# A diffusion trunk's layer on one core: the queries made beside the q/kv projection, in areas shared with its input

## The chip, the cores and the metric

One core of a Trainium2 chip runs the whole program. The time is device microseconds from start to end of one execution; the median of several runs is what is compared. The profile is one more execution, recorded by the hardware profiler. Engines: TensorE (PE, matmuls; its weight loads are listed as PEld), VectorE (DVE), ScalarE (ACT), GpSimd (POOL) and SyncE (SP, which issues nearly all DMAs). Each engine runs its own list of instructions in order and waits for others at semaphores.

## The reference

One layer for 1024 latent tokens and 128 context tokens (9 tiles of 128 tokens, 8 of them latent), width 1024. The tokens are normalised and modulated to `h`, one input projection feeds two groups of heads, and the part that matters here is the second, a latent attention with 4 heads:

```python
h = _rmsnorm(x, norm_g) * (1 + scale) + shift
u, v, g_a, c_q, c_kv, k_rope, g_b = _split_in(h @ w_in)
...
q = (_rmsnorm(c_q, q_norm_g) @ w_uq).reshape(B, L, MLA_HEADS, QK_NOPE + QK_ROPE)
ckv = _rmsnorm(c_kv, kv_norm_g)
...
logits.append(jnp.einsum('bqhn,bkhn->bhqk', qn, kn) + jnp.einsum('bqhr,bkr->bhqk', qrb, kr))
```

`c_q` has 256 columns, `c_kv` 128 and `k_rope` 64: together the 448 columns of the q/kv projection. Everything is computed in float32.

## The kernel before

The work runs in stages. **Front:** `x` is transposed and modulated; `hh` and `hl` hold the result, tokens in columns, by block `k` of 128 channels (8) and group `g` of three token tiles (384 columns). Each float32 matmul is done in three passes, for which a matrix is split into a part rounded for the fast format (`..h`, by ACT or POOL) and the rest (`..l`, by DVE, `lo_of`, L105). **Channel stage:** twelve blocks of the input projection for the gates and the first group of heads. **q/kv projection** (from L804 on): for each token tile `t` the 24 matmuls of L812 to L814 make `zacc` in one PSUM bank. `z_stats` (L767) then has ACT square (L772, L773) and copy it (L774), DVE work out the reciprocal root in some fifteen operations on two columns (L776, L777, then `rsqrt`, L115 to L125) and POOL rotate the key part. `cq_transpose` (L797) brings the previous tile's `c_q` to columns and `fold` (L746, tiles 2 to 5) multiplies two query weights of a head into one. **Query stage** (from L829 on): `q_nope(g, h)` (6 matmuls of 384 columns), `q_rope(t)` (6 of 256), `q_rope_T(t)` (4 transposes) and `keys` (transposes of key tiles) write the query areas `q` and the key tiles. **Attention** (from L953 on) and the **output projection** follow.

From the query stage on, the order on each engine is the program's own: a block under `tc.manual_schedule` keeps the order in which the instructions are written. `run` executes a step's matmuls at once and moves a counted clock on by the step's cost; `later(dt, fn)` sets an eviction aside until that clock has passed `dt`, and `need` brings it forward when a step depends on it. So the costs in the code only set the order. The q/kv loop before is not under such a block.

PSUM has 8 banks: `psa` hands out six in turn (tag "acc": `zacc`, `qn`, `qr`, some `qrT`), `pst` two (tag "t": `cqT`, `fold`, `kT`, other `qrT`). A step that takes a bank waits until the bank's last user has been read out.

In SBUF `hh` and `hl` are 48 tiles of 384 columns in the pool `ht`. When the q/kv projection is done the pool is closed, and three query pools of the same size in sum (`qp0` to `qp2`) and the key pool `kv` are opened in its place and in that of `w1`. Late in the attention, `qp0` makes room for a pool `wo` with the first pieces of the output weights and the tiles `mh`, `ml` of the output stage; the other pieces lie in `qp1` and `qp2`.

```python
for t in range(NT):
    ...
    z_stats(t, ps)
    if FT <= t < FT + 4:
        fold(t - FT)
    if t > 0:
        cq_transpose(t - 1)
```

Of the kernel before, what the change touches and what calls it, by code (L numbers as in the profile page):

```python
# [9 lines left out]
F32 = mybir.dt.float32  # L10
# [77 lines left out]
def tile_hymba_step(ctx: ExitStack, tc: tile.TileContext, I, O):  # L88
# [115 lines left out]


# [540 lines left out]
    def fold(h):  # L746
# [20 lines left out]
    def z_stats(t, ps):  # L767
# [3 lines left out]
        j1 = sm.tile([P, 256], BF16, tag="j1", name=f"j1{t}", bufs=1)  # L771
        S.activation(j1, ps[:, 0:256], AF.Square, accum_out=ssz[:, 0:1])  # L772
        S.activation(j1[:, :128], ps[:, 256:384], AF.Square, accum_out=ssz[:, 1:2])  # L773
        S.copy(zs, ps[:, :448])  # L774
        v = sm.tile([P, 2], F32, tag="zv", name=f"zv{t}")
        V.tensor_scalar(v[:, 0:1], ssz[:, 0:1], 1.0 / 256.0, EPS, op0=ALU.mult, op1=ALU.add)  # L776
        V.tensor_scalar(v[:, 1:2], ssz[:, 1:2], 1.0 / 128.0, EPS, op0=ALU.mult, op1=ALU.add)  # L777
        r = rsqrt(sm, v, 2, "z")
        V.tensor_scalar(scl[:, t : t + 1], r[:, 0:1], ATTN_SCALE, None, op0=ALU.mult)
        V.tensor_scalar(nscl[:, t : t + 1], r[:, 0:1], -ATTN_SCALE, None, op0=ALU.mult)  # L780
        V.scalar_tensor_tensor(kvn[:, t, :], zs[:, 256:384], r[:, 1:2], kvg, op0=ALU.mult, op1=ALU.mult)
        kr = zs[:, 384:448]
        if t < NS:
# [22 lines left out]
    for t in range(NT):  # L806
# [9 lines left out]
        if FT <= t < FT + 4:  # L816
            fold(t - FT)
# [716 lines left out]
```

## Time and profile before

| | us |
|---|---|
| Median of 3 runs (lowest, highest) | 637.11 (632.85, 637.33) |
| Profiled execution, its own time | 638.64 |
| Span of the profile | 636.9 |
| Busy: PE, DVE, ACT, POOL | 616.1, 361.3, 256.0, 186.3 |

The profiled execution's own time is 1.7 us longer than its span: what lies before the first and after the last instruction. Matmuls are pipelined and their ends are modelled, so two of them overlap in the list, and the start of one to the start of the next is its pitch. The q/kv projection starts at 253.4 us, the query stage at 300.5 and the scores at 330.7. An `idle before` names what released the engine. [...]

### The profile page before, as it was taken

What the parts mean: (1) busy time and instruction counts of PE and PEld (TensorE: products, weight loads), DVE (VectorE), ACT (ScalarE), POOL (GpSimd) and SP (SyncE); (2) the same over time, 40 slices, a digit from 0 to 9 for tenths busy, and PEclk for the clock granted to TensorE, in tenths of its full rate; (3) what the DMA queues carried; (4) which work ended last, traced back from release to release, by engine and by line L of the source; (5) the groups of instructions that cost most, each with busy time, mean ns of one, the idle gap of its engine ahead of it and who ended that gap; (6) DMA issues with size and microseconds to landing.
All of it is one profiled execution on the core that took longest, in us unless ns stands there. A gap on an engine that the chain in (4) does not pass through costs nothing.

```text
span 636.9 us, 9914 instructions
## 1 busy us (share of the span) xinstructions
PE 616.1 (97%) x3715; PEld 557.1 (87%) x3715; DVE 361.3 (57%) x922; ACT 256.0 (40%) x613; POOL 186.3 (29%) x219
## 2 busy tenths in 40 slices
PE   7799999999999999999979999999999999999995
PEld 6577889999999999999968899999999988888884
DVE  4427446236866200566876666777667765387655
ACT  4355784012111111333765655555655542232222
POOL 3534202355436510222753222332222341000001
PEclk9799999999999999999989999999999999999998
DMA  8866200015023430000000000001101112523311
GB/s 321 331 229 217 66 1 2 1 42 205 20 97 113 127 116 0 25 15 1 7 2 1 1 1 9 26 1 35 34 1 34 33 67 69 198 99 133 105 61 66
DMA packets 17119, 46.32 MB, mean 73 GB/s; under 512 B 1952, under 2 KB 6448, under 8 KB 17072
## 3 DMA queue, kind: packets, MB, share of 16 engines
q1 hardware_dynamic: 16928, 45.51, 20.6%
q8 instruction: 29, 0.48, 0.3%
q10 hardware_dynamic: 144, 0.20, 0.1%
q14 instruction: 18, 0.15, 0.1%
HBM read 40.87 MB, written 4.83 MB: 72 GB/s over the span
## 4 chain that ended last, share of the span: by engine, by line
PE 89%; DVE 3%; DMA 2%; issue 2%; ACT 2%; SPq 1%; POOL 0%; ACTq 0%; DVEq 0%
PE tp L618 6%; PE tp L151 6%; PE tp L152 6%; PE tp L153 6%; PE pT L1046 5%; PE w L1303 5%; PE w L1304 5%; PE w L1305 5%; PE s L999 3%; PE s L1000 3%; PE s L1002 3%; PE o L1072 3%; PE s L1001 3%; PE o L1070 3%; PE s L1003 3%; PE o L1071 3%
## 5 line engine op out<-in xcount | busy, mean ns | idle before, releaser
L990 POOL TENSOR_SCALAR e<-e,rs 128x1280 f32<-128x1280 f32 x32 | 42.8, 1339 | 139.4 <-DVE rs L989 123.7
L105 DVE TENSOR_TENSOR pl<-pT,ph 128x512 fp32r<-128x512 f32 x81 | 55.5, 687 | 47.6 <-ACT ph L1050 47.4
L153 PE MATMUL tp<-hh,w2l 128*128 128x384 f32 x216 | 72.6, 336 | 0.0
L152 PE MATMUL tp<-hl,w2h 128*128 128x384 f32 x216 | 72.6, 336 | 0.0
L151 PE MATMUL tp<-hh,w2h 128*128 128x384 f32 x216 | 72.6, 336 | 0.0
L984 ACT ACTIVATE e<-s,nb,scl 128x256 f32<-128x256 f32 x64 | 56.1, 881 | 39.2 <-DVE nb L978 39.1
L1050 ACT CAST ph<-pT 128x512 fp32r<-128x512 f32 x80 | 45.4, 589 | 44.0 <-PE pT L1046 39.0
L1046 PE MATMUL pT<-ident,e 128*128 128x128 f32 x320 | 47.9, 273 | 0.7 <-DVE pl L105 0.7
L1070 PE MATMUL o<-ph,vh 128*128 128x256 f32 x160 | 47.3, 296 | 0.0
L105 DVE TENSOR_TENSOR w2l<-w2r,w2h 128x1024 fp32r<-128x1024 f32 x12 | 20.2, 1687 | 43.8 <-POOL w2h L108 43.8
L1072 PE MATMUL o<-ph,vl 128*128 128x256 f32 x160 | 44.7, 279 | 0.0
L1071 PE MATMUL o<-pl,vh 128*128 128x256 f32 x160 | 44.6, 278 | 0.0
L999 PE MATMUL s<-kch,q 128*128 128x512 f32 (+2 forms) x100 | 39.5, 395 | 2.1 <-DVE q L105 2.1
L974 DVE TENSOR_REDUCE m<-s 128x1 f32<-128x1024 f32 x32 | 38.9, 1216 | 4.4 <-PE s L1003 4.4
L1046 PEld LDWEIGHTS pT<-ident,e 128*128 128x128 f32 x320 | 37.5, 140 | 4.4 <-DVE pl L105 1.5
L151 PEld LDWEIGHTS tp<-hh,w2h 128*128 128x128 f32 x216 | 40.6, 188 | 0.6
L152 PEld LDWEIGHTS tp<-hl,w2h 128*128 128x128 f32 x216 | 40.6, 188 | 0.2
L153 PEld LDWEIGHTS tp<-hh,w2l 128*128 128x128 f32 x216 | 40.6, 188 | 0.0
L1000 PE MATMUL s<-kcl,q 128*128 128x512 f32 (+2 forms) x100 | 35.9, 359 | 0.0
L1002 PE MATMUL s<-krh,q 128*128 128x512 f32 (+2 forms) x100 | 35.7, 357 | 0.0
L1001 PE MATMUL s<-kch,q 128*128 128x512 f32 (+2 forms) x100 | 35.7, 357 | 0.0
L1003 PE MATMUL s<-krl,q 128*128 128x512 f32 (+2 forms) x100 | 35.5, 355 | 0.0
(301 smaller groups left out, 1620.0 us busy)
## 6 DMA issues: line engine op xcount, KB each, us to landing
ada<-in_ada_ss SPq DMA_DIRECT2D x16, 512.0 KB, 11.1
w2r<-in_w_t SPq DMA_DIRECT2D x12, 512.0 KB, 3.8
xr<-in_x SPq DMA_DIRECT2D x9, 512.0 KB, 4.9
adag<-in_ada_g SPq DMA_DIRECT2D x8, 512.0 KB
wor<-in_w_o SPq DMA_DIRECT2D x8, 512.0 KB, 3.2
out_y<-y SPq DMA_DIRECT2D x8, 512.0 KB, 3.1
x<-in_x SPq DMA_DIRECT2D x6, 512.0 KB, 8.7
wvr<-in_w_v SPq DMA_DIRECT2D x8, 256.0 KB, 7.4
```

The costliest lines, as they stand in the source:

```text
L105: V.tensor_tensor(lo, src, f32(hi), op=ALU.subtract)
L151: T.matmul(ps, wh, xh, start=j == 0, stop=False)
L152: T.matmul(ps, wh, xl, start=False, stop=False)
L153: T.matmul(ps, wl, xh, start=False, stop=j == n - 1)
L984: S.activation(e[:, sl], src, AF.Exp, bias=nb, scale=scl[:, t : t + 1], accum_out=su[:, i : i + 1])
L999: T.matmul(ps, qh_, kch[:, sl], start=True, stop=False)
L1000: T.matmul(ps, qh_, kcl[:, sl], start=False, stop=False)
L1001: T.matmul(ps, ql_, kch[:, sl], start=False, stop=False)
L1046: T.transpose(ps[:, w : w + P], es[t, h][:, c * P : (c + 1) * P], ident)
L1070: T.matmul(o, vh[:, kt, :], ph[:, sl], start=c == 0, stop=False)
L1071: T.matmul(o, vh[:, kt, :], pl[:, sl], start=False, stop=False)
L1072: T.matmul(o, vl[:, kt, :], ph[:, sl], start=False, stop=c == n - 1)
```

## The change

Three tiles `area0` to `area2` replace the 48 tiles: `hh[k, g]` and `hl[k, g]` are columns of `area[g]`, and the queries of group `g` are written over them, once the q/kv projection has read the three tiles of the group. The query pools are gone, and the output weights and `mh` later lie in the same areas. The q/kv loop is put under `manual_schedule` and cut into eight steps of three matmuls (`z_chunk`); `merged` deals a second list in between by cost: `q_rope(t - 2)`, one or two `q_nope`, `cq_transpose(t - 1)`, `fold(t - 1)` (tiles 1 to 4), `q_rope_T(t - 3)`. What is left runs after the loop in a written order. In `z_stats` the copy comes ahead of the squares, and all of it is set aside by `later`. The warm-up of Exp's table (`warm_e`) is no longer tied to its place behind the query stage.

```diff
-    hh, hl = {}, {}
-    for k in range(NK):
-        for g in range(3):
-            hh[k, g] = ht.tile([P, GW], F32R, tag=f"hh{k}{g}", name=f"hh{k}{g}")
-            hl[k, g] = ht.tile([P, GW], F32R, tag=f"hl{k}{g}", name=f"hl{k}{g}")
+    area = [ht.tile([P, 16, GW], F32R, tag=f"area{g}", name=f"area{g}") for g in range(3)]
+    hh = {(k, g): area[g][:, 2 * k, :] for k in range(NK) for g in range(3)}
+    hl = {(k, g): area[g][:, 2 * k + 1, :] for k in range(NK) for g in range(3)}
...
+        def copies():
+            j1 = sm.tile([P, 256], BF16, tag="j1", name=f"j1{t}", bufs=1)
+            S.copy(zs, ps[:, :448])
+            S.activation(j1, ps[:, 0:256], AF.Square, accum_out=ssz[:, 0:1])
+            S.activation(j1[:, :128], ps[:, 256:384], AF.Square, accum_out=ssz[:, 1:2])
...
+        later(0.3, copies)
+        later(0.9, rope_key)
+        later(1.6, scales)
...
-        q = qpool[g].tile([P, 4, 4, GW], F32R, tag="q", name=f"q{g}")
+    for g in range(3):
+        q = area[g].rearrange("p (s h) c -> p s h c", s=4)
         qnh[g], qnl[g], qr[g] = q[:, 0], q[:, 1], q[:, 2:4]
...
+    NOPES = {4: [(0, 0)], 5: [(0, 1), (0, 2)], 6: [(0, 3)], 7: [(1, 0), (1, 1)], 8: [(1, 2), (1, 3)]}
     with tc.manual_schedule(engines=engines):
...
+        warm_e = sm.tile([P, 1], F32, tag="warm", name="warm_e", bufs=1)
+        S.activation(warm_e, ones[:, 0:1], AF.Exp)
+        rope_weights()
+        for t in range(NT):
+            beside = []
             if t >= 2:
-                run((0.43, lambda: q_rope_T(t - 2)))
...
+                beside.append((0.75, lambda t=t: q_rope(t - 2)))
+            beside += [(1.05, lambda n=n: q_nope(*n)) for n in NOPES.get(t, [])[:1]]
+            if t >= 1:
+                beside.append((0.25, lambda t=t: cq_transpose(t - 1)))
+            if 1 <= t < 5:
+                beside.append((0.45, lambda t=t: fold(t - 1)))
+            if t >= 3:
+                beside.append((0.45, lambda t=t: q_rope_T(t - 3)))
+            beside += [(1.05, lambda n=n: q_nope(*n)) for n in NOPES.get(t, [])[1:]]
+            merged([(0.62, lambda t=t, k=k: z_chunk(t, k)) for k in range(NK)], beside)
+        closed(c_w1)
+        c_kv, kv = opened("kv", side="left")
...
+        for cost, fn in (
+            (0.45, lambda: keys(0, 4, 0)),
+            (0.75, lambda: q_rope(7)),
+            (0.45, lambda: keys(0, 4, 1)),
+            (0.45, lambda: q_rope_T(6)),
+            (0.25, lambda: cq_transpose(8)),
+            (0.45, lambda: keys(4, 4, 0)),
+            (0.45, lambda: keys(4, 4, 1)),
+            (0.75, lambda: q_rope(8)),
+            (1.05, lambda: q_nope(2, 0)),
+            (0.45, lambda: q_rope_T(7)),
+            (1.05, lambda: q_nope(2, 1)),
+            (0.15, lambda: keys(8, 1, 1)),
+            (1.05, lambda: q_nope(2, 2)),
+            (0.15, lambda: keys(8, 1, 0)),
+            (1.05, lambda: q_nope(2, 3)),
+            (0.25, lambda: q_rope_T(8)),
+        ):
+            run((cost, fn))
         catch_up(1e9)
-    warm_e = sm.tile([P, 1], F32, tag="warm", name="warm_e", bufs=1)
-    tc.keep_in_program_order(S.activation(warm_e, ones[:, 0:1], AF.Exp))
...
-            mh[t] = wo.tile([P, 8, P], F32R, tag="mh", name=f"mh{t}", bufs=2)
+            mh[t] = flat[0][4 + len(mh) % 2].rearrange("p (c q) -> p c q", c=8)
```

Here is PE's list at the head of token tile 3 before the change (a name's first number is its tile; `hh01` is block 0 of group 1):

```order
L812 MATMUL zacc3_2634<-qh0_1654,hh01_114 128x448
L813 MATMUL zacc3_2634<-ql0_1655,hh01_114 128x448
L814 MATMUL zacc3_2634<-qh0_1654,hl01_115 128x448
L812 MATMUL zacc3_2634<-qh1_1786,hh11_120 128x448
L813 MATMUL zacc3_2634<-ql1_1787,hh11_120 128x448
L814 MATMUL zacc3_2634<-qh1_1786,hl11_121 128x448
```

And the same place after it:

```order
L937 MATMUL zacc3_2589<-qh0_1609,area1_113 128x448
L938 MATMUL zacc3_2589<-ql0_1610,area1_113 128x448
L939 MATMUL zacc3_2589<-qh0_1609,area1_113 128x448
L151 MATMUL qr1_2600<-wrh_2377,cqh_2373 128x256 [waits Activation_49]
L152 MATMUL qr1_2600<-wrl_2378,cqh_2373 128x256
L153 MATMUL qr1_2600<-wrh_2377,cql_2374 128x256 [waits DVE_49]
```

`q_rope(1)` (`qr1`, six matmuls, three shown) has moved from the query stage to behind the first three matmuls of tile 3, and with it a wait for DVE's `cql`.

PE's list at the end of the query stage, before (`qn23` is `q_nope` of group 2, head 3; `s100` the first scores):

```order
L151 MATMUL qn23_3413<-cqh_2418,wfh_2420 128x384
L152 MATMUL qn23_3413<-cql_2419,wfh_2420 128x384
L153 MATMUL qn23_3413<-cqh_2418,wfl_2421 128x384
L888 MATMUL qrT8_3424<-ident_75,qun8_3371 128x128 [waits DVE_49,PE_49,Activation_49]
L888 MATMUL qrT8_3424<-ident_75,qun8_3371 128x128
L999 MATMUL s100_3453<-kch_3061,q0_3067 128x512 [waits DVE_49]
L1000 MATMUL s100_3453<-kcl_3062,q0_3067 128x512
```

PE's list behind the first keys and `q_rope(7)` of the new tail (`kT00`, `kT01` are the two kinds of key tiles 0 to 3, `kT40`, `kT41` of 4 to 7):

```order
L917 MATMUL kT01_3243<-ident_75,krd_2386 128x128 [waits PE_49]
L917 MATMUL kT01_3243<-ident_75,krd_2386 128x128 x3
L897 MATMUL qrT6_3260<-ident_75,qr16_3133 128x128 [waits Pool_49]
L897 MATMUL qrT6_3260<-ident_75,qr16_3133 128x128
L897 MATMUL qrT6_3260<-ident_75,qun6_3119 128x128 x2
L836 MATMUL cqT8_3268<-ident_75,z8_3200 128x128 [waits DVE_49]
L836 MATMUL cqT8_3268<-ident_75,z8_3200 128x128
L917 MATMUL kT40_3273<-ident_75,kvn_2385 128x128 [waits DVE_49]
L917 MATMUL kT40_3273<-ident_75,kvn_2385 128x128 x3
L917 MATMUL kT41_3285<-ident_75,krd_2386 128x128 [waits DVE_49]
L917 MATMUL kT41_3285<-ident_75,krd_2386 128x128 x3
```

The keys, which stood among `q_nope` and `q_rope` before, now follow each other and `cqT8`; `kT01`, `cqT8`, `kT40` and `kT41` take the two banks of `pst` in turn, the last three with a wait for DVE.

DVE's list where the second keys are read out, before (`zr`, `scl`, `kvn` belong to the statistics of tile 8):

```order
L105 TENSOR_TENSOR kcl_3062<-kT00_3103,kch_3061 128x512 [waits Activation_49]
L125 SCALAR_TENSOR_TENSOR zr_3015<-zt_3016,zr_3015 128x2 [waits DVE_49]
L872 TENSOR_TENSOR qr11_3130<-qr1_3109,rope_2424 128x256 [waits Activation_49]
L779 TENSOR_SCALAR scl_92<-zr_3015 128x1 [waits DVE_49]
L780 TENSOR_SCALAR nscl_93<-zr_3015 128x1
L781 SCALAR_TENSOR_TENSOR kvn_2436<-z8_3006,zr_3015,kvg_162 128x128
L105 TENSOR_TENSOR q0_3067<-qn02_3121,q0_3067 128x384 [waits Activation_49]
L105 TENSOR_TENSOR krl_3064<-kT01_3136,krh_3063 128x512 [waits Activation_49]
```

And after:

```order
L124 TENSOR_TENSOR zt_3237<-zt_3237,zw_3238 128x2 [waits DVE_49]
L105 TENSOR_TENSOR krl_3209<-kT01_3243,krh_3208 128x512 [waits Activation_49]
L125 SCALAR_TENSOR_TENSOR zr_3236<-zt_3237,zr_3236 128x2 [waits DVE_49]
L123 TENSOR_TENSOR zt_3237<-zr_3236 128x2 [waits DVE_49]
L907 TENSOR_TENSOR area2_114<-qrT6_3260,area2_114 64x4x128 [waits PE_49,Activation_49]
L105 TENSOR_TENSOR cql_2374<-cqT8_3268,cqh_2373 128x2x128 [waits PE_49]
```

Before, the statistics of tile 8 end ahead of `krl`; now six of their operations stand between `kcl` and `krl` and two more behind `krl`, ahead of a half of `q_rope_T(6)`'s read-out and of `cql`.

## Rows read from the trace of the kernel before

**Rows 1.** Page, part 1: busy time, share of the span, instructions of each engine

```profile
PE 616.1 (97%) x3715; PEld 557.1 (87%) x3715; DVE 361.3 (57%) x922; ACT 256.0 (40%) x613; POOL 186.3 (29%) x219
```

**Rows 2.** Windows: length, busy us (instructions) of each engine, PE clock, DMA share, GB/s

```profile
260.00:300.00 40.00, 40.00 (x213) 37.22 (x212) 26.09 (x148) 12.79 (x52) 10.90 (x40) 1.00 0.06 16
300.00:320.00 20.00, 19.94 (x143) 19.06 (x142) 16.83 (x45) 15.85 (x38) 13.88 (x28) 1.00 0.02 6
320.00:340.00 20.00, 16.10 (x91) 13.95 (x91) 14.01 (x26) 10.38 (x22) 7.02 (x11) 0.91 0.00 1
```

**Rows 3.** Timeline of PE, 324 to 335: start, us, engine, line, operation [idle before <-releaser]

```profile
324.41 0.34 PE L153 MATMUL qn<-cqh,wfl 128*128 128x384 f32 x1
326.25 0.41 PE L888 MATMUL qrT<-ident,qr 128*128 128x128 f32 x2 [1.50 <-DVE q L898]
...
327.60 0.34 PE L153 MATMUL qn<-cqh,wfl 128*128 128x384 f32 x1
328.25 0.41 PE L888 MATMUL qrT<-ident,qun 128*128 128x128 f32 x2 [0.31 <-DVE q L898]
330.74 0.57 PE L999 MATMUL s<-kch,q 128*128 128x512 f32 x1 [2.08 <-DVE q L105]
...
334.48 0.39 PE L1003 MATMUL s<-krl,q 128*128 128x512 f32 x1
334.71 0.28 PE L999 MATMUL s<-kch,q 128*128 128x256 f32 x1
```

**Rows 4.** Windows, PE alone, 331 to 332: length, busy, granted clock, DMA

```profile
331.00:332.00 1.00, 1.00 (x4) 0.51 0.00 0
```

**Rows 5.** Timeline of PE, end of token tile 0 and the query stage

```profile
258.10 0.37 PE L814 MATMUL zacc<-qh,hl 128*128 128x448 f32 x1
258.31 0.36 PE L812 MATMUL zacc<-qh,hh 128*128 128x448 f32 x1
...
311.88 0.36 PE L151 MATMUL qr<-wrh,cqh 128*128 128x256 f32 x1
...
312.68 0.34 PE L151 MATMUL qn<-cqh,wfh 128*128 128x384 f32 x1
...
313.73 0.27 PE L907 MATMUL kT<-ident,kvn 128*128 128x128 f32 x1
...
314.19 0.36 PE L151 MATMUL qr<-wrh,cqh 128*128 128x256 f32 x1
```

**Rows 6.** Timeline of ACT, first token tile's statistics

```profile
258.51 0.38 ACT L772 ACTIVATE j<-zacc 128x256 bf16<-128x256 f32 x1 [4.39 <-PE zacc L814]
...
259.28 0.53 ACT L774 COPY z<-zacc 128x448 f32<-128x448 f32 x1
259.69 0.52 ACT L761 ACTIVATE wrh<-rraw,cst 128x256 fp32r<-128x256 f32 x1
```

**Rows 7.** Groups by line, DVE, 253.4 to 331: count, busy us, mean ns, idle before

```profile
L898 DVE TENSOR_TENSOR q<-qrT,q 64x512 fp32r<-64x512 f32 x16 | 11.0, 689 | 0.4
...
L123 DVE TENSOR_TENSOR zt<-zr 128x2 f32<-128x2 f32 x27 | 5.7, 212 | 0.9
...
L105 DVE TENSOR_TENSOR cql<-cqT,cqh 128x256 fp32r<-128x256 f32 x9 | 3.8, 418 | 0.4
...
L105 DVE TENSOR_TENSOR kcl<-kT,kch 128x512 fp32r<-128x512 f32 x2 | 1.4, 681 | 0.0
```

**Rows 8.** Groups by line, ACT, the same stretch

```profile
L910 ACT CAST kch<-kT 128x512 fp32r<-128x512 f32 x2 | 1.2, 587 | 0.0
```

**Rows 9.** Timeline, table load, end of the first exponential, third head's scores

```profile
329.45 1.28 ACT L952 ACT_TABLE_LOAD   x1
...
330.75 0.20 ACT L952 ACTIVATE warm_e<-ones 128x1 f32<-128x1 f32 x1
...
338.40 0.20 ACT L984 ACTIVATION_READ_ACCUMULATOR e<-s,nb,scl 128x1 f32 x1
...
340.46 0.40 PE L999 MATMUL s<-kch,q 128*128 128x512 f32 x1
```

More of the change, by code (lines that the diff above doesn't have):

```diff
@@ L203, in run, with merged @@
         now[0] += step[0]
+    def merged(a, b):
+        ta, tb = sum(x for x, _ in a) or 1.0, sum(x for x, _ in b) or 1.0
+        ia = ib = 0
+        da = db = 0.0
+        while ia < len(a) or ib < len(b):
+            if ib >= len(b) or (ia < len(a) and da / ta <= db / tb):
+                da += a[ia][0]
+                run(a[ia])
+                ia += 1
+            else:
+                db += b[ib][0]
+                run(b[ib])
+                ib += 1
     c_pc, pc = opened("pc", side="right")
@@ L876, in raw @@
             made.add(("r", t))
-        later(0.75, raw)
+        later(0.85, raw)
     def q_rope_T(t):
@@ L883, in q_rope_T @@
         srcs = rot[t]
-        tp = (pst if t >= TP else psa).tile([P, 512], F32, tag="t" if t >= TP else "acc", name=f"qrT{t}")
+        late = t == NS
+        tp = (pst if late else psa).tile([P, 512], F32, tag="t" if late else "acc", name=f"qrT{t}")
         for s_, src in enumerate(srcs):
@@ L931, in tile_hymba_step @@
[L931 to L949 removed]
+        pool_copy(vh[:, vs_, :], kvn[:, vs_, :])
@@ new lines, in values, with z_chunk @@
+        G.tensor_tensor(vl[:, vs_, :], kvn[:, vs_, :], f32(vh[:, vs_, :]), op=ALU.subtract)
+    zps = {}
+    def z_chunk(t, k):
+        g, j = t // 3, t % 3
+        sl = slice(j * P, (j + 1) * P)
+        if k == 0:
+            zps[t] = psa.tile([P, 512], F32, tag="acc", name=f"zacc{t}")
+        ps = zps[t]
+        a, b = hh[k, g][:, sl], hl[k, g][:, sl]
+        T.matmul(ps[:, :448], a, wqh[k], start=k == 0, stop=False)
+        T.matmul(ps[:, :448], a, wql[k], start=False, stop=False)
+        T.matmul(ps[:, :448], b, wqh[k], start=False, stop=k == NK - 1)
+        if k == NK - 1:
+            z_stats(t, ps)
@@ L1093, in value_steps @@
         return ns, tr, av, fin1, fin2
-    def merged(a, b):
-        ta, tb = sum(x for x, _ in a) or 1.0, sum(x for x, _ in b) or 1.0
-        ia = ib = 0
-        da = db = 0.0
-        while ia < len(a) or ib < len(b):
-            if ib >= len(b) or (ia < len(a) and da / ta <= db / tb):
-                da += a[ia][0]
-                run(a[ia])
-                ia += 1
-            else:
-                db += b[ib][0]
-                run(b[ib])
-                ib += 1
     woh, wol = {}, {}
+    flat = []
+    for g in range(3):
+        cols = area[g].rearrange("p a c -> p (a c)")
+        flat.append([cols[:, n * 1024 : (n + 1) * 1024] for n in range(6)])
     his, los = [], []
@@ L1317, in tile_hymba_step @@
             if 2 * c + LEAD + 1 == 11:
[L1318 removed]
                 c_wo, wo = opened("wo", side="left")
                 for k in range(2):
[L1321 removed]
+                    wo_piece(k, *flat[0][2 * k : 2 * k + 2])
                 mix_jobs(8)
```

183 lines of the change are left out of this document (72 added, 111 removed).

## The prediction, as written before the changed kernel was run

> **What bounds the kernel now.** Read the page first: TensorE (PE) is busy 97% of the span, the vector engine (DVE) 57% [rows 1]. So a change that keeps PE's work can give back only time in which PE waits or runs slowly. The windows say where that is in the stages the change touches: in 260 to 300 us PE is never idle and DVE is busy 26.1 of 40 us; in 300 to 320 DVE rises to 16.8 of 20; in 320 to 340 PE is idle 3.9 us and its granted clock falls to a mean of 0.91 [rows 2]. The timeline of PE, last, gives the places and, in brackets, what ended each wait: DVE's subtractions (L898, L105) all three times. I count from start to start, since ends are modelled. A query matmul has a pitch of 1.05/6 = 0.175 (six from 312.68 to 313.73 [rows 5]), a transpose 0.46/5 = 0.092 (five from 313.73 to 314.19). The gaps [rows 3]:
> 324.41 to 326.25 is 1.84, less 0.175: 1.66 waited.
> 327.60 to 328.25 is 0.65, less 0.175: 0.48.
> 328.25 to 330.74 is 2.49, less two transposes: 2.31.
> Sum 4.45 us. Then the first ten score matmuls, 330.74 to 334.71, take 3.97 us, though the tenth takes 0.23 (334.48 to 334.71), so ten should take 2.3: 1.67 us lost. [...] Everything that this change can win is thus 4.45 + 1.67 = 6.1 us, 1.0% of the span. [...]
>
> **What the change removes.** Eight of the twelve q_nope, seven of the nine q_rope and six of the nine q_rope_T go in front, between the q/kv matmuls. PE's instructions are the same ones, so PE's own work is unchanged. DVE's work is spread: a tile of the new loop holds on PE 24 q/kv matmuls at 0.21 (258.10 to 258.31 [rows 5]), one q_rope (0.80, 311.88 to 312.68), two q_nope (2.1) and six transposes (0.55), 8.5 us; on DVE some 15 small operations at 0.2, a rotation of 256 columns (taken as the 256-column row, 0.42), two q_nope subtractions (bounded by 0.42 and 0.68 of the 256- and 512-column rows), cql 0.42 and two rotation subtractions at 0.69 [rows 7]: about 6.3 us. DVE keeps up there. The three waits above therefore go, 4.45 us.
>
> **What it adds: waits in the new tail.** After the last q/kv matmul PE still has six key transposes, q_rope 7 and 8, the q_nope of group 2 and three q_rope_T. The order shows three of these waiting for DVE through the two transposing banks (pst). Let T be the start of keys(0,4,0).
> ScalarE (ACT): the last q/kv matmul starts at T - 0.21, its copy 0.41 later (258.10 to 258.51 [rows 5, 6]), at T + 0.20. The copy now stands first (259.28 to 259.69, 0.41) and the two squares behind it (258.51 to 259.28, 0.77), so the cast of the first keys starts at T + 1.38 and ends at 1.97 (0.587 [rows 8]). DVE's kcl takes 0.681 [rows 7]: T + 2.65. PE got there at 0.37 + 0.80 + 0.37 + 0.37 = 1.91, so cq_transpose(8), which needs that bank, waits 0.74.
> DVE goes on in its order: rotation of q_rope(7) 0.42 (3.07), six small operations of tile 8's statistics at 0.2 (4.27), krl 0.68 (4.95). keys(4,4,0) needs that bank; PE was ready at 2.65 + 0.18 = 2.83 and waits 2.12.
> Then two small operations (5.35), half a rotation subtraction 0.69 (6.04), cql 0.42 (6.46). keys(4,4,1) waits for it; PE was ready at 4.95 + 0.37 = 5.32 and waits 1.14.
> Sum 4.0 us. Behind the waiting PE stand q_rope(8) and four q_nope, then the scores; by then (some 6 us of PE work later) DVE has the bank of the first scores free, so nothing is added there. I bound this sum from below at 0.7 (only the first wait, if the small operations slip in while DVE waits for ACT) and from above at 5.5 (ACT another 1.5 us late) and take 4.0, since every term is a row.
>
> **Other edits.** cq_transpose(0) comes after 3 matmuls of tile 1: PE is there 0.84 after the last matmul of tile 0 starts, the copy ends 0.41 + 0.53 = 0.94 after it [rows 5, 6], a wait of 0.1. The folds move one tile ahead; their loads stand on SP in the same order and behind the same buffers, freed by the q/kv weight splits of the stage before, so they cost nothing unless such a load is late; then the first fold would wait for it. The shared areas are followed by region: the writes of the input wait for the same instructions as before, and the queries of a group are written after its three tiles. Context and values on POOL go behind the tail, and are wanted only by the scores' third part and the value product: hidden. The Exp warm-up is hoisted to ACT's first instruction, where Silu's load then evicts it, so the 1.28 us load at 329.45 goes to the first exponential of the softmax [rows 9]. There the end of that exponential (338.40 + 0.20 = 338.60) had 1.86 us before the third head's scores at 340.46 that reuse its bank. The load fits: 0.
> [...]
>
> **The sum.** Waits 4.45 fall to 4.1: 0.35 us. And the clock? The new tail waits 4.0 of the 4.55 us from T + 1.91 to T + 6.46, at least as long and as dense as the stretch that ended in the window at 0.51 [rows 3, 4]. I take it that the clock falls again, only over q_rope(8) and q_nope instead of over the scores: 1.67 lost there as here.
> [...]
> So the profiled execution would go from 638.64 (636.9 of span and 1.7 around it) to 638.3. That execution lies 1.5 above the median; on the median the forecast is 637.11 - 0.35, about 636.8.
>
> **Rivals.**
> No dip: same waits, but the clock stays at full, because two groups of transposes break them. For it: the wait of 1.66 at 324 was not followed by slow work (326.25 to 327.60 holds four transposes and five query pitches, 0.37 + 0.88, at about full pace [rows 3]). Against it: the density above. 636.8 - 1.7 = 635.1.
> No late tail: ACT and DVE, freed of the backlog, have their casts ready, and only the 0.1 and the 0.7 stay. For it: DVE is busy only 26 of 40 us before [rows 2]. Against it: the chain cast, subtraction, bank is a latency, and an idle DVE does not shorten it. 637.11 - 6.1 + 0.8 = 631.8.
> Late third head: the Exp load in the softmax takes more than its 1.28 us, so that the 1.86 us in hand are overdrawn. At twice the row that is 2.56 - 1.86 = 0.7 us, 637.5. For it: nothing in the trace. Against it: an operation follows its load at once (329.45 + 1.28 to 330.75 [rows 9]). [...]
> Slower: DVE's subtraction of the transposed cq stands behind tile statistics (15 small operations and one longer, 3.0 us), and q_rope at the head of the tile after next waits for it. Place: tile 7, where 9 matmuls and 4 transposes lie between, 2.2 us, for 0.41 + 0.41 + 0.42 of eviction, a margin of 1.0; elsewhere (12 matmuls, a q_nope, 4 transposes: 3.9) 2.6. It decides from where DVE is over 1.0 us behind. Price if it is behind by one whole chain: 2.0 there and 0.4 in four other tiles, 3.6. For it: the engines keep their program order. Against it: 6.3 us of DVE work in 8.5. 636.8 + 3.6 = 640.4.
> That nothing is interleaved is excluded by the order.
>
> **Chances.** Forecast 0.42, no dip 0.25, no late tail 0.15, late third head 0.03, slower 0.15. The three runs before lie from 632.85 to 637.33, 0.7% apart, so 1% (6.4 us) is about what a measurement can tell from no change. For the range: the low end takes in the rival at 631.8 with 0.8 us for such scatter, 631.0; the high end stops at 639.6, which leaves most of the slower rival, some 0.1, outside. Faster by over 1% needs under 630.7: only a part of the no-late-tail case, 0.06. Slower by over 1% needs over 643.5: more than one chain late, 0.04. Between: 0.90.
>
> **What would show it.** Right: PE waits at cq_transpose(8), keys(4,4,0) and keys(4,4,1) of about 0.7, 2.1 and 1.1 us, released by DVE; no wait at the first score; the window behind them at the 0.5 level and the first scores at a pitch of 0.23; the Exp load ahead of the first exponential, with no wait of the third head. Wrong: waits of q_rope in the loop, released by DVE's cql; tail waits under 1 us; or an attention stage that has grown.

## The result, and the profile after

The changed kernel is slower: 640.11 us median of 20 runs (636.51 to 641.19) beside 637.46 of the kernel before (20 runs). The ratio is 1.0043 (95% interval 1.0027 to 1.0059), +2.7 us (1.7 to 3.8). It was forecast at 636.8, range 631.0 to 639.6: the time lies above that range, and the sign is the other one. The profiled execution took 639.19 us, with a span of 637.4.

Page, part 1, of the changed kernel (answers to [rows 1]):

```profile
PE 616.1 (97%) x3715; PEld 557.5 (87%) x3715; DVE 367.3 (58%) x922; ACT 259.3 (41%) x614; POOL 186.3 (29%) x219
```

PE's busy time is the same to the tenth of a microsecond (it counts matmuls at half clock at their longer time, four transposes 0.60 us at 315.88 and 1.12 at 324.71 below, so it is no measure of the work), and so is its count. DVE's 922 instructions are as many as before, and yet they take 6.0 us more. That is the first trace of what happened; at this point it says only that some of DVE's operations have become longer, not which.

Windows of the changed kernel, in the stretches of [rows 2]:

```profile
260.00:300.00 40.00, 40.00 (x233) 37.56 (x233) 28.57 (x124) 19.12 (x56) 14.65 (x40) 1.00 0.04 11
300.00:320.00 20.00, 18.51 (x113) 17.17 (x111) 16.03 (x57) 11.31 (x32) 8.38 (x23) 1.00 0.00 0
320.00:340.00 20.00, 16.40 (x89) 14.90 (x90) 15.60 (x31) 8.82 (x19) 7.22 (x11) 0.83 0.09 32
```

The loop works as intended: PE has no idle time in 260 to 300. The loss is behind 316, where the loop has ended. The granted clock of 320 to 340 is 0.83, where it was 0.91.

Timeline of PE at the end of the stage (answers to [rows 3, 5]; columns as there):

```profile
315.88 0.60 PE L917 MATMUL kT<-ident,kvn 128*128 128x128 f32 x4
...
317.69 0.38 PE L897 MATMUL qrT<-ident,qun 128*128 128x128 f32 x2
319.39 0.44 PE L836 MATMUL cqT<-ident,z 128*128 128x128 f32 x2 [1.32 <-DVE kcl L105]
322.38 1.12 PE L917 MATMUL kT<-ident,kvn 128*128 128x128 f32 x4 [2.55 <-DVE krl L105]
324.71 1.12 PE L917 MATMUL kT<-ident,krd 128*128 128x128 f32 x4 [1.22 <-DVE cql L105]
325.48 0.56 PE L151 MATMUL qr<-wrh,cqh 128*128 128x256 f32 x1
...
333.12 0.47 PE L1044 MATMUL s<-kch,area 128*128 128x512 f32 x1
...
335.48 0.28 PE L1044 MATMUL s<-kch,area 128*128 128x256 f32 x1
```

The three waits stand exactly where they were forecast, with the forecast releasers, but they are longer. From start to start, less the transposes between at 0.092: 1.52, 2.81 and 1.96 us, 6.3 in all, where 0.74, 2.12 and 1.14 (4.0) were expected. Of the third, some 0.4 us is the clock: transposes then run at the lower level, and the next four take 0.77 (324.71 to 325.48) instead of 0.37. Without that the waits are 5.9. The first ten score matmuls are now at full pace (333.12 to 335.48, 2.36 us). What lies ahead of them is not: windows of the changed kernel,

```profile
322.00:324.00 2.00, 1.12 (x4) 0.72 (x4) 1.94 (x4) 0.47 (x1) 1.83 (x4) 0.56 0.00 0
324.00:326.00 2.00, 1.29 (x6) 1.29 (x7) 1.90 (x5) 0.25 (x2) 1.92 (x3) 0.50 0.03 8
...
328.00:330.00 2.00, 2.00 (x12) 1.90 (x11) 1.51 (x3) 0.90 (x2) 0.00 (x0) 0.74 0.11 26
```

The clock is at its lower level, 0.50, from about 322 to 329.

### The profile page after: what moved, and what is told of

The parts are those of the page before. It is cut to its first block, busy times and chain, and to the rows that moved or that the text cites. A ratio compares the mean times of both kernels' runs of the same rounds, so it can differ in the third digit from the quotient of the medians.

```text
span 637.4 us, 9898 instructions
## 1 busy us (share of the span) xinstructions
PE 616.1 (97%) x3715; PEld 557.5 (87%) x3715; DVE 367.3 (58%) x922; ACT 259.3 (41%) x614; POOL 186.3 (29%) x219
## 4 chain that ended last, share of the span: by engine, by line
PE 90%; DVE 3%; DMA 2%; ACT 2%; issue 1%; SPq 1%; POOL 0%; ACTq 0%
PE tp L153 6%; PE tp L632 6%; PE tp L151 6%; PE tp L152 6%; PE pT L1091 5%; PE w L1340 5%; PE w L1339 5%; PE w L1338 5%; PE s L1044 3%; PE o L1117 3%; PE o L1115 3%; PE s L1045 3%; PE o L1116 3%; PE s L1047 3%; PE s L1048 3%; PE s L1046 3%
## 5 line engine op out<-in xcount | busy, mean ns | idle before, releaser
L153 PE MATMUL tp<-area,w2l 128*128 128x384 f32 x216 | 72.6, 336 | 0.0
L152 PE MATMUL tp<-area,w2h 128*128 128x384 f32 x216 | 72.6, 336 | 0.0
L151 PE MATMUL tp<-area,w2h 128*128 128x384 f32 x216 | 72.6, 336 | 0.0
L1340 PE MATMUL w<-area,ml 128*128 128x512 f32 (+1 forms) x114 | 43.2, 379 | 0.0
L151 PEld LDWEIGHTS tp<-area,w2h 128*128 128x128 f32 x216 | 40.6, 188 | 0.6
L152 PEld LDWEIGHTS tp<-area,w2h 128*128 128x128 f32 x216 | 40.6, 188 | 0.2
L153 PEld LDWEIGHTS tp<-area,w2l 128*128 128x128 f32 x216 | 40.6, 188 | 0.0
L1044 PE MATMUL s<-kch,area 128*128 128x512 f32 (+2 forms) x100 | 39.2, 392 | 0.0
L632 PE MATMUL tp<-area,w2h 128*128 128x384 f32 x144 | 37.0, 339 | 0.0
L1045 PE MATMUL s<-kcl,area 128*128 128x512 f32 (+2 forms) x100 | 35.5, 355 | 0.0
L1047 PE MATMUL s<-krh,area 128*128 128x512 f32 (+2 forms) x100 | 35.3, 353 | 0.0
```

The source lines that it names most:

```text
L151: T.matmul(ps, wh, xh, start=j == 0, stop=False)
L152: T.matmul(ps, wh, xl, start=False, stop=False)
L153: T.matmul(ps, wl, xh, start=False, stop=j == n - 1)
L632: T.matmul(tps[i, g][:, :GW], w_[i][:, k, :], x_[k, g], start=k == 0 and j == 0, stop=k == NK - 1 and j == 2)
L1044: T.matmul(ps, qh_, kch[:, sl], start=True, stop=False)
L1340: T.matmul(ps, b, woh[k][:, c0:c1], start=False, stop=k == NK - 1)
```

## Where the chain got its extra time

Read DVE and POOL side by side over the tail. DVE of the changed kernel, 317 to 324 (two-column operations are the last tile's statistics; kcl, krl and cql are what PE waits for):

```profile
317.65 0.68 DVE L115 TENSOR_SCALAR zt<-zv 128x2 int32<-128x2 int32 x1
...
318.66 0.68 DVE L105 TENSOR_TENSOR kcl<-kT,kch 128x512 fp32r<-128x512 f32 x1
...
319.84 0.71 DVE L124 TENSOR_TENSOR zt<-zt,zw 128x2 f32<-128x2 f32 x1
320.58 0.33 DVE L125 SCALAR_TENSOR_TENSOR zr<-zt,zr 128x2 f32<-128x2 f32 x1
320.94 0.16 DVE L123 TENSOR_TENSOR zt<-zr 128x2 f32<-128x2 f32 x1
321.14 0.59 DVE L124 TENSOR_TENSOR zt<-zt,zw 128x2 f32<-128x2 f32 x1
321.65 0.68 DVE L105 TENSOR_TENSOR krl<-kT,krh 128x512 fp32r<-128x512 f32 x1
322.25 0.67 DVE L125 SCALAR_TENSOR_TENSOR zr<-zt,zr 128x2 f32<-128x2 f32 x1
322.95 0.54 DVE L123 TENSOR_TENSOR zt<-zr 128x2 f32<-128x2 f32 x1
```

POOL of the changed kernel at the same time:

```profile
317.58 0.72 POOL L975 TENSOR_TENSOR kcl<-ctxr,kch 128x256 fp32r<-128x256 f32 x1
...
319.81 0.72 POOL L883 TENSOR_TENSOR qr<-qr,qr 128x256 f32<-128x256 f32 x1 [0.68 <-DVE zt L123]
320.50 0.40 POOL L108 TENSOR_SCALAR krh<-ctxr 128x256 fp32r<-128x256 f32 x1
320.99 0.72 POOL L975 TENSOR_TENSOR krl<-ctxr,krh 128x256 fp32r<-128x256 f32 x1
...
322.16 0.73 POOL L975 TENSOR_TENSOR vl<-ctxr,vh 128x256 fp32r<-128x256 f32 x1
322.87 0.61 POOL L108 TENSOR_SCALAR vh<-kvn 128x512 fp32r<-128x512 f32 x1
```

An operation on two columns takes 0.16 us when POOL is idle (L124 at 302.73 in the kernel before, for one), and here 0.33 to 0.71. Add start and duration: L115 ends at 318.33, POOL's subtraction at 318.30; the first L124 at 320.55, POOL at 320.53; then 320.91 and 320.90, 321.73 and 321.71, 322.92 and 322.89, 323.49 and 323.48. Each long one ends 0.01 to 0.03 us behind the operation that POOL was in. The subtractions kcl and krl, whose source lies in PSUM, keep their 0.68 beside POOL, as in [rows 7]. Against 0.16 (0.17 for the two integer operations L115 and L116, of which L116, 0.38 long, is not shown) the statistics ahead of cql lost 0.51 + 0.21 + 0.55 + 0.17 + 0.43 + 0.51 + 0.38 = 2.8 us.

The theory after this reading (P): the tail's waits are the forecast ones, plus what POOL's conversions of context and values cost the small operations of DVE beside them. Rivals: the small operations are slow for a reason of their own (O); the waits are DVE's program order (O'); the half clock is the larger part (C); the place of the Exp load costs something after all. The rows above speak for P: each of the six long operations starts 0.03 to 0.15 us behind POOL's and ends 0.01 to 0.03 behind it. What ties the two ends together, they do not show.

## The experiments

To compare stages I use distances in the timeline of PE: the start of the first q/kv matmul, from there to the start of the eleventh score matmul (the stage that the change rewrites), from there to the end. A profile's distances repeat well, its front does not, so the middle column is the sharpest measure; the ratio, from 10 to 20 executions of each kernel beside the kernel before, is what counts in the end. Where a row has no ratio, the kernel was executed once.

| kernel | first q/kv matmul at | to the eleventh score | to the end | ratio to before, 95% interval |
|---|---|---|---|---|
| before | 253.43 | 81.28 | 302.19 | 1 |
| before once more | 251.48 | 81.29 | 302.13 | one execution |
| changed | 252.22 | 83.26 | 301.92 | 1.0043 (1.0027 to 1.0059) |
| POOL late | 250.38 | 80.21 | 301.91 | 0.9992 (0.9968 to 1.0016) |
| statistics behind | 251.72 | 80.70 | 301.98 | 0.9990 (0.9962 to 1.0018) |
| waits filled | 250.78 | 81.76 | 301.96 | 1.0012 (0.9986 to 1.0038) |
| Exp behind | 253.95 | 83.59 | 301.96 | 1.0034 (1.0009 to 1.0059) |
| POOL and statistics | 251.46 | 78.85 | 301.89 | 0.9966 (0.9946 to 0.9986) |
| tail in other banks | 250.49 | 80.47 | 301.94 | 0.9978 (0.9961 to 0.9995) |
| statistics early | 252.14 | 78.64 | 301.92 | 0.9969 (0.9946 to 0.9991) |
| POOL's pairs back | 254.50 | 81.51 | 302.19 | 1.0026 (0.9999 to 1.0053) |
| POOL's copies back | 253.33 | 81.20 | 302.17 | one execution |
| statistics between | 253.35 | 77.39 | 301.96 | 0.9969 (0.9946 to 0.9993) |

**POOL late.** From the changed kernel, POOL's conversions moved behind the last tile's statistics: the values of tile 8, which wait for those, now stand first.

```diff
-        for dh, dl, i in (
...
-            later(0.5 + i, lambda dh=dh, i=i: pool_copy(dh, ctxr[:, i, :]))
...
-            later(3.6 + 2 * n, lambda t0=t0, c=c: values(t0, c))
+        def pool_tail():
+            values(8, 1)
...
+            values(0, 4)
+            values(4, 4)
...
+        later(4.4, pool_tail)
```

> Only the place of GpSimd's (POOL's) eleven-odd conversions of context and values changes: they go behind the last tile's statistics instead of beside them. Theory P (POOL beside VectorE lengthens VectorE's small operations on SBUF operands, 0.16 us alone and 0.54 to 0.71 in the tail of the changed kernel, and the waits are the forecast 4.0 us plus that): the small operations fall to about 0.16 to 0.2, the three waits of TensorE from 5.9 us (1.5, 2.8, 1.5) to about 4.0 (0.7, 2.1, 1.1), and the time from 640.1 to about 638.2. Rival O (the small operations are slow for a reason of their own, such as their place behind ScalarE): their durations, the waits and the time stay, 640.1 within 0.5.

Measured: ratio 0.9992, 3.2 us below the changed kernel's; the stage fell by 3.05 us. DVE in that run, its statistics ahead of krl:

```profile
315.77 0.17 DVE L115 TENSOR_SCALAR zt<-zv 128x2 int32<-128x2 int32 x1
...
317.00 0.28 DVE L117 TENSOR_SCALAR zw<-zv 128x2 f32<-128x2 f32 x1
...
317.37 0.70 DVE L124 TENSOR_TENSOR zt<-zt,zw 128x2 f32<-128x2 f32 x1
318.10 0.16 DVE L125 SCALAR_TENSOR_TENSOR zr<-zt,zr 128x2 f32<-128x2 f32 x1
...
318.57 0.68 DVE L105 TENSOR_TENSOR krl<-kT,krh 128x512 fp32r<-128x512 f32 x1
```

and what POOL did in it between 317 and 322:

```profile
317.33 0.72 POOL L883 TENSOR_TENSOR qr<-qr,qr 128x256 f32<-128x256 f32 x1
321.50 0.30 POOL L108 TENSOR_SCALAR vh<-kvn 128x128 fp32r<-128x128 f32 x1 [3.45 <-DVE kvn L808]
```

Only two operations are longer than alone, and both met POOL's last rotation: the 0.70 its sum (317.33 to 318.05; it ends at 318.07), the 0.28 the product ahead of that. PE in that run:

```profile
314.00 0.60 PE L917 MATMUL kT<-ident,kvn 128*128 128x128 f32 x4
...
316.81 0.44 PE L836 MATMUL cqT<-ident,z 128*128 128x128 f32 x2 [0.62 <-DVE kcl L105]
319.31 0.87 PE L917 MATMUL kT<-ident,kvn 128*128 128x128 f32 x4 [2.07 <-DVE krl L105]
320.75 1.11 PE L917 MATMUL kT<-ident,krd 128*128 128x128 f32 x4 [0.56 <-DVE cql L105]
...
328.21 0.47 PE L1048 MATMUL s<-kch,area 128*128 128x512 f32 x1
```

With T the start of the first key transposes, the three waits end at T + 2.81, 5.31 and 6.75. The prediction had T + 2.65, 4.95 and 6.46; the changed kernel has T + 3.51, 6.50 and 8.83. So P holds, and O does not: the small operations fall to 0.16 in the same place behind ACT. The waits are 0.82, 2.32 and 1.07 by start to start, 4.2 against 4.0 forecast. What I had not expected is the other microsecond: the stage gained 3.05 us, the waits only 2.1. The rest is clock: windows show it below 1.00 from 318 to 324 only (means 0.70 and 0.74), some 3.4 us at the lower level where the changed kernel has 6.8. The second of these windows:

```profile
322.00:324.00 2.00, 2.00 (x12) 2.00 (x11) 1.46 (x3) 0.86 (x2) 1.83 (x5) 0.74 0.20 49
```

**Statistics behind.** The last tile's statistics come behind cql on DVE; POOL stays beside them.

```diff
-        later(1.6, scales)
+        later(1.6 if t < NS else 3.7, scales)
```

> Only the last tile's statistics move: on VectorE they come behind the subtraction of the transposed cq (cql) instead of between kcl and cql. Theory O' (what TensorE waits for is VectorE's program order, some nine small operations ahead of krl and cql): waits of about 0.7, 0.9 and 0.7 us by the rows, 2.4 in all instead of 5.9, and a shorter stretch at half clock, so 640.1 - 3.5 to 640.1 - 5: 635 to 636.6. Rival (the waits are a latency of cast, subtraction and bank, whatever stands between): waits of 4 us or more and a time within 1 us of 640.1.

Measured: 0.9990, 3.4 us below the changed kernel, just short of what was expected, with the clock at full pace throughout the tail (q_nope at a pitch of 0.175 us). The waits at the three places are 0.82, 0.74 and 1.39 by start to start, 2.95 in all. But two new ones appear at the end of the tail, behind the moved statistics:

```profile
327.25 0.30 PE L917 MATMUL kT<-ident,kvn 128*128 128x128 f32 x1 [1.34 <-DVE kvn L808]
329.48 0.44 PE L897 MATMUL qrT<-ident,qun 128*128 128x128 f32 x2 [0.85 <-DVE krl L105]
```

So O' is a cause beside P: the operations cost PE something because they stand ahead of krl and cql, and beside POOL they cost more.

**Waits filled.** PE gets matmuls in the three waits; they read finished operands, and nothing reads their result.

```diff
+            (0.0, lambda: filler(8)),
             (0.25, lambda: cq_transpose(8)),
+            (0.0, lambda: filler(14)),
             (0.45, lambda: keys(4, 4, 0)),
+            (0.0, lambda: filler(10)),
             (0.45, lambda: keys(4, 4, 1)),
```

> TensorE gets 32 more matmuls of 384 columns, 8, 14 and 10 of them ahead of the three instructions that wait, whose result is never read. Theory C (the half clock behind the waits costs about 2.3 us: 324.71 to 333.12 is 8.4 us for work that takes 6.1 at full pace): the clock stays at 1.00 through the tail, the three instructions start where they did, within 0.3 us, and the time falls to about 637.8 although 32 matmuls are added. Rival (the half clock is not caused by the waits, or costs nothing): the time stays at 640.1 or rises.

Measured: 1.0012, 2.0 us below the changed kernel, with 32 matmuls more. The intervals of the two overlap; the stage, 1.50 us shorter, is the firmer sign. The clock stays at 1.00 in every window of the tail. PE in that run:

```profile
318.13 2.68 PE L984 MATMUL filler<-cqh,wfh 128*128 128x384 f32 x14
320.96 0.66 PE L917 MATMUL kT<-ident,kvn 128*128 128x128 f32 x4
...
323.30 0.66 PE L917 MATMUL kT<-ident,krd 128*128 128x128 f32 x4
```

The last of the three starts 8.89 us after the first key transposes (314.41), as in the changed kernel (8.83), so the waits are the same. What follows takes 6.86 us to the first score instead of 8.41. The clock alone was thus worth 1.55 us, less than the 2.3 expected, in part because a faster PE then met a wait for DVE at the last query transpose (0.4 us from start to start).

**Exp behind.** The warm-up of the exponential's table stands behind the tail again, as before the change.

```diff
+    warm_e = sm.tile([P, 1], F32, tag="warm", name="warm_e", bufs=1)
+    tc.keep_in_program_order(S.activation(warm_e, ones[:, 0:1], AF.Exp))
```

> Only the Exp warm-up is put back behind the query stage, as in the kernel before. If its load (1.28 us) is hidden in the softmax of the first head, as forecast: 640.1 within 0.5. Rival (the load ahead of the first exponential delays the heads behind it): 640.1 less 0.7 to 1.3, 638.8 to 639.4.

Measured: 1.0034, too near both sides to part them by the time alone; but behind the eleventh score it takes 301.96 us where the changed kernel has 301.92: nothing, as forecast. In the changed kernel (answers to [rows 9], timeline of ACT):

```profile
337.57 1.28 ACT L1029 ACT_TABLE_LOAD   x1 [3.49 <-DVE nb L1023]
338.87 0.56 ACT L1029 ACTIVATE e<-s,nb,scl 128x256 f32<-128x256 f32 x1
```

The load stands in front of the first exponential, takes 1.28 us, and the exponential follows 0.02 us later. The hoisted warm-up had its own load at 0.73, and the first Silu's at 2.59 came behind it. The third head's scores start 5.76 us after the eleventh score matmul (335.48 to 341.24), before 5.75 (334.71 to 340.46).

**POOL's pairs back, POOL's copies back.** Both start from the run with POOL late and put work on POOL where context and values had stood, whose result nobody reads: 14 subtractions of two SBUF operands, or 20 conversions of one.

```diff
+        idle = zp.tile([P, 128], F32R, tag="idle", name="idle")
+        for i in range(14):
+            later(0.5 + 0.22 * i, lambda: G.tensor_tensor(idle, ctxr[:, 0, 0:128], ctxr[:, 1, 0:128], op=ALU.subtract))
```

> The run with POOL late, plus 14 subtractions of 128 columns on POOL (two operands in SBUF, a result never read, about 0.45 us each) at the place where context and values stood. Theory P (POOL's activity as such lengthens VectorE's small operations beside it): these rise again from 0.16 to 0.5 and more, the waits from 4.0 to 5 or more, first key transpose to first score from 14.2 to 15.5 to 17.5 us, and the time by 2 to 3 us, to about the changed kernel's. Rival (it was what the context and values wrote or read, or their order against VectorE's instructions): small operations at 0.16 and 14.2 us.

Measured: 1.0026, and 15.5 us from the first key transposes to the first score where POOL late has 14.2. Some of the small operations beside the pairs rise to 0.32 to 0.45, about a pair's length, others stay at 0.14 to 0.17; beside POOL's rotation, which POOL late has too, they take 0.30 to 0.57. One of each engine, the pairs as a block of ten:

```profile
323.07 0.38 DVE L124 TENSOR_TENSOR zt<-zt,zw 128x2 f32<-128x2 f32 x1
```

```profile
322.98 5.25 POOL L984 TENSOR_TENSOR idle<-ctxr 128x128 fp32r<-128x128 f32 x10
```

The waits rise with them, to 5.1 us from start to start:

```profile
321.20 0.44 PE L836 MATMUL cqT<-ident,z 128*128 128x128 f32 x2 [0.89 <-DVE kcl L105]
324.10 0.66 PE L917 MATMUL kT<-ident,kvn 128*128 128x128 f32 x4 [2.47 <-DVE krl L105]
325.74 1.12 PE L917 MATMUL kT<-ident,krd 128*128 128x128 f32 x4 [0.98 <-DVE cql L105]
```

So it is POOL's activity and not what becomes of its result: the pairs read the context, as the conversions did, but nothing waits for what they write. The sizes lie at the short end of what P asked for; that these pairs are 0.45 us long and not 0.72 would account for it, but was not tested. The stage is 1.3 us longer than in POOL late; the intervals of the two ratios overlap.

```diff
+        for i in range(20):
+            later(0.5 + 0.155 * i, lambda: pool_copy(idle, ctxr[:, 0, 0:128]))
```

> The run with POOL late, plus 20 conversions of 128 columns on POOL with one operand (a result never read, about 0.3 us each) at the same place. If any operation of POOL on SBUF does it: the small operations of VectorE rise to about 0.3 to 0.5 and first key transpose to first score to 15 us or more. If only operations with two operands do: 0.16 and 14.2 us.

Measured, in one execution: neither outcome. The first five two-column operations beside the conversions take 0.15 to 0.21, two later ones 0.26 (0.16 alone) and 0.48 (128 columns, 0.35 alone), and the waits end at T + 2.80, 5.14 and 6.58, no later than in POOL late. Yet the first score comes at T + 15.15, as if the conversions had held DVE up. The windows say why: the clock is at 0.50 from 322 to 328, about 6.8 us in all. One of these windows, T + 9 to 11 (that of POOL late above is T + 8 to 10):

```profile
326.00:328.00 2.00, 2.00 (x8) 1.90 (x8) 0.55 (x1) 0.44 (x2) 1.67 (x6) 0.50 0.08 17
```

So 0.9 us came from the clock alone, at equal waits. Conversions of 128 columns hardly hold DVE up (0.26 us at most for two columns); those of 256 and 512 columns did in the changed kernel (0.33 and 0.54 above). Where between them it begins was not tried.

**POOL and statistics.** Both edits at once; the first two context pieces go ahead of the tail.

```diff
-        later(1.6, scales)
+        later(1.6 if t < NS else 3.7, scales)
...
+        context(*ctxs[0])
+        context(*ctxs[1])
+        later(6.2, pool_tail)
```

> Both earlier edits at once: the last tile's statistics behind cql, and POOL's values and the third context piece behind those statistics (the first two context pieces ahead of the tail, where VectorE reads PSUM). If place in VectorE's order and POOL are two causes: the waits of the run with the statistics behind (0.6, 0.5, 1.1, then 1.3 and 0.9 at the last key transpose and the last query transpose) lose their last two, since those came from small operations of 0.54 to 0.69 us beside POOL; first key transpose to first score 14.7 - 2 = 12.7 us, where the run with POOL late alone has 14.2; time about 638.1 x 0.9990 - 2 = 635.5. Rival (one cause seen twice: either edit alone already gives all there is): 14.2 to 14.7 us and 637 to 637.6.

Measured: 0.9966 (0.9946 to 0.9986), 635.72 us: faster than before and than the changed kernel; 12.9 us to the first score, where 12.7 was expected, and a clock of 1.00 throughout. P and O' are two causes, and each edit gives something that the other leaves. They do not add up in full: the stage is 4.4 us shorter than the changed kernel's, where the edits alone gave 3.05 and 2.56. Either edit shortens the stretch at half clock, from 6.8 us to 3.4 and to none, and that is gained only once.

**Tail in other banks, statistics early, statistics between.** Three tries to take the rest. In the first, cq_transpose(8) comes third and in an accumulator bank, and the last tile's squares and statistics come late; in the second they come early; in the third behind krl. All three also move POOL's conversions further back, two more steps of PE's list and some read-outs; only the lines that matter most are shown, each against the run before it.

```diff
+            (0.25, lambda: cq_transpose(8)),
             (0.45, lambda: keys(0, 4, 1)),
...
+                later(3.2, lambda: squares(zs))
```

> As the run before, and the tail in another order: the transpose of the last cq ahead of the second key transposes and in an accumulator bank (psa), its cast and subtraction ahead of the rotation's, the squares of the last tile behind, read from the copy in SBUF. If the waits for VectorE through the two transposing banks are all that is left: no wait above 0.5 us, clock 1.00 throughout, first key transpose to first score about 8.6 us of TensorE's work and up to 1 of waits, 9 to 9.6, against 17.2 in the changed kernel: 7.6 to 8.2 us off its 640.9 beside this before, 632.7 to 633.3, faster than before by 5 us. Rival (the waits only move, to the first scores that need banks and context that VectorE and POOL now give later): 12 us or more to the tenth score matmul plus later stages longer than 302.2, and a time above 635.

Measured: 0.9978. The three waits are gone and the clock is full to the last q_nope, but PE then waits 2.0 us for the scaled keys of tile 8 and 1.5 for the subtraction behind them, and the first scores run at half clock (0.73 on the mean of 328 to 332). Not the 5 us expected: the waits only moved, as the rival had it (16.6 us to the tenth score, 636.4 us), though to the last transposes and not to the first scores, and the later stages did not grow (301.94).

```diff
-                later(3.2, lambda: squares(zs))
+                later(1.95, lambda: squares(zs))
```

> As the run with the tail in another order, and the last tile's squares and statistics come earlier, in the 1.7 us in which VectorE was idle there; the last query transpose takes an accumulator bank. If the two waits left (2.0 for the last tile's scaled keys, 1.5 for the subtraction behind it) and the half clock of 1.4 us in the first scores behind them are that chain alone: both waits under 0.7 us, the tenth score at 11.5 to 12.5 us after the first key transpose (16.6 there), clock 1.00, time 636.4 - 4 = 632 to 633. Rival (VectorE's work of the tail, some 13 us beside 8.6 of TensorE's, is simply too much, so that a wait comes back elsewhere): 14 us or more, 635 or more.

Measured: 0.9969, 634.41 us. Those two waits went, and one of 2.0 us for krl came, with 3.4 us of half clock behind it (q_nope at a pitch of 0.32 us until 325.57): ScalarE's squares now stood ahead of its cast, and six of VectorE's statistics ahead of krl itself, one of them 0.70 us long beside POOL's rotation. The wait came back elsewhere, as the rival had it (14.8 us to the tenth score); the time lies between the two sides.

```diff
-                later(1.95, lambda: squares(zs))
+                later(2.75, lambda: squares(zs))
```

> As the run with the statistics early, but ScalarE's squares and VectorE's first statistics come behind the second key pieces (krh, krl) instead of ahead of them. If the wait of 2.0 us for krl there came from that place alone: it goes, the scaled keys of the last tile come by 8 us after the first key transpose, and the tenth score at 11.5 to 13 us (14.8 there), time about 634.4 - 2 = 632 to 633. Rival (VectorE's 13 us of work in the tail simply move the wait again): 14 us or more, and no faster than 634.4 beside the same before.

Measured: 0.9969 (0.9946 to 0.9993), 634.60 us. In its profile the stage is the shortest, 77.39 us, 3.9 less than before, with the clock at full pace (q_nope at a pitch of 0.175 us), and two waits marked in PE's list:

```profile
326.38 0.30 PE L931 MATMUL kT<-ident,kvn 128*128 128x128 f32 x1 [0.49 <-DVE kvn L814]
...
328.37 0.47 PE L1066 MATMUL s<-kch,area 128*128 128x512 f32 x1 [1.48 <-DVE area L921]
```

The ratio shows some 2 us of it (0.4 to 3.4). The tenth score matmul starts 13.5 us after the first key transposes, between the two sides of the expectation, and the ratio is that of the run with the statistics early: the wait for krl went with the place of the squares and statistics ahead of it, and another took part of its room. That last one, 1.48 us, is for a subtraction of DVE ahead of the first score, as the rival had it.

**Before once more.**

> The kernel before once more, for the scatter of one profile. If the stretch that the change touches is the same in each execution: 81.3 us within 0.4 from the first q/kv matmul to the tenth score, and 302.4 within 0.3 from there to the end, while the start of the first q/kv matmul may differ from 253.4 by up to 2. Rival (the stretch itself scatters by 1 us or more, so that single profiles of it say nothing): outside of these.

Measured, to the eleventh score as in the table (the expectation calls it the tenth): 81.29 and 302.13, against 81.28 and 302.19; the front ends at 251.48 instead of 253.43. The stage of the kernel before repeats to 0.1 us. That of the changed kernel has no repeat; the run with Exp behind, whose stage differs only in the warm-up, has 0.33 us more, so allow as much. The front, whose instructions the change leaves as they are but for the warm-up, ends between 250.4 and 254.5 in these profiles, and goes with the clock: it is at 0.50 for 6.8 us of the front in the three that end by 250.8, for 10.2 us in eight (251.5 to 253.4), for 13.7 us in the two that end at 253.95 and 254.50 (the clock's mean over the whole execution is 0.990 to 0.991, 0.983 to 0.989 and 0.981 to 0.982). Of the changed kernel's +2.7 us (1.7 to 3.8) the two profiles show 83.26 + 301.92 - 81.28 - 302.19 = 1.7 us in the stage and the rest. The other 1.0 is not traced: the front scatters by more than that, and whether it is longer on the mean is not shown.

## Why the prediction was wrong, point by point

- **What bounds the kernel, and what goes.** Right. The three waits and the slow first scores of [rows 3, 4] are gone, and nothing in the loop took their place: PE is busy 63.99 of 64.00 us between 253 and 317; from start to start there is one wait, 0.18 us at cq_transpose(0) (257.50 to 257.88, less 0.20), where 0.1 was forecast. That DVE keeps up beside the q/kv matmuls held; so did the 0 for folds, areas and the Exp load. So of the rivals, no late tail, no dip, the late third head (5.76 us against 5.75) and the waits of q_rope in the loop did not happen. The last gave 640.4, next to the measured 640.11; that is luck, since it came out by another mechanism.
- **The places of the new waits.** Right, all three, with their releasers.
- **Their size.** This is the step that failed. The sum had "six small operations of tile 8's statistics at 0.2" and, under other edits, "Context and values on POOL go behind the tail, and are wanted only by the scores' third part and the value product: hidden". On POOL they stand behind the last tile's rotary key and wait for nothing there, so POOL does them at once, beside the small operations; and these I had priced by a mean whose operations fall mostly in a stage in which POOL worked 10.9 of 40 us [rows 2]. Measured: the six took 2.1 us instead of 1.2, the two behind krl 1.2 instead of 0.4, and two more ahead of kcl (L115, L116), which the sum did not have, 0.7 more than alone; 6.3 us of waits instead of 4.0, above the upper bound of 5.5 too, which allowed only for a late ACT. With POOL out of the way the same chain gave 4.2. I asked whether POOL's results are wanted early; the question that was missing is what else POOL's work holds up.
- **Why before did not pay for it.** There POOL converts the context in the query stage, from 305.3 to 312.2. The last tile's statistics end at 307.5, so only the first piece meets them, and PE does not wait for DVE before 324. Most of the conversions run beside DVE's subtractions from PSUM, which POOL does not slow (512 columns: 0.68 us at 310.21, beside POOL, and 0.68 at 321.84 of the run with the statistics early, where POOL is idle). The trace of before had the mechanism in view; its timelines of DVE and POOL hold this pair, which ends at 305.35 and 305.34:

```profile
304.76 0.59 DVE L123 TENSOR_TENSOR zt<-zr 128x2 f32<-128x2 f32 x1
```

```profile
304.60 0.74 POOL L875 TENSOR_TENSOR qr<-qr,qr 128x256 f32<-128x256 f32 x1
```

I read the group of [rows 7] by its mean, 212 ns, which hides that most of the 27 operations take 0.16 to 0.17 (median 165 ns) and one 0.59.
- **The clock.** Right that it falls again. The size: 1.67 was assumed, from the first scores of the kernel before, where the clock is at 0.50 from 331.0 to 334.4; 1.55 came back by filling the waits, less what a new wait took. By subtraction the changed kernel loses more. From first key transposes to first score it takes 17.24 us. By the pitches of [rows 5] the work in it is 4.2 (four q_nope), 1.6 (two q_rope) and 30 transposes at 0.092, 2.8, together 8.6. Less that and 6.3 of waits, 2.3 are left (2.7 beside the waits of 5.9). The half clock lasts 6.8 us there.
- **The sum.** Waits +1.8 (6.3 for 4.45), clock +0.6 (2.3 for 1.67), the attention stage -0.3: 2.1 by these, 1.7 found. The 0.4 between is PE's time in the new loop, which I did not take apart. With POOL late the stage comes to 80.21, near the 80.9 that the forecast implies, and the time to 0.9992 (0.9968 to 1.0016) of before where 0.9995 was forecast. The waits of that kernel are the forecast ones to 0.2 us; that the time agrees as well says less, its interval being wider than the whole forecast change.

## What to carry to other kernels

An engine whose results nobody needs yet is not free: here VectorE's tiny operations on two columns in SBUF could last until the GpSimd operation beside them had ended (0.33 to 0.71 us instead of 0.16), where that had two operands or was a conversion of 256 or 512 columns. So look for chains of such operations that someone waits for, and keep them away from bulk conversions on GpSimd, or let these wait for the chain's end. Price an operation by a row in which the neighbouring engines do what they will do in its new place. And when interleaving empties a stage's end of its cover, look at what is last: the last tile's statistics had work around them before, and in the new tail they are on the path.

## What the runs showed of the hardware

- A VectorE operation on 128 x 2 elements in SBUF took 0.14 to 0.17 us alone and up to 0.71 beside GpSimd, ending 0.01 to 0.03 us behind GpSimd's operation in the six rows above; one on 128 x 128 elements (kvn) 0.35 alone and 1.48 beside a subtraction of 1.29. The longer times stand at operations of one SBUF operand (L115 0.68, L116 0.38) as well as of two. One-column operations with a single tensor operand took 0.14 to 0.16 in all the timelines of DVE, beside POOL too (0.14 at 306.81 of the kernel before), and 512-column subtractions from PSUM stayed at 0.68. Conversions of 128 columns on POOL lengthened the two-column operations by 0.1 us at most, in one execution.
- The stretch at half clock is not set by the waits alone: with three waits of the same size it lasted 3.4 us with POOL late and 6.8 with POOL's copies back, which is 0.9 us of time. Filling the waits with matmuls that nobody reads kept the clock at 1.00 in every window of the tail, and the stage became 1.50 us shorter.
